# A hybrid decoder layer on one core: another place for the row of -M, for four blocks of weights and for the outputs' pool

## The chip, the core and the metric

The kernel runs on one NeuronCore of a Trainium2 chip. The core has a matrix engine (TensorE, in the profile PE, its weight loads PEld), a vector engine (VectorE, DVE), an engine for functions and copies (ScalarE, ACT), a small general engine (GpSimd, POOL) and one that issues transfers (SyncE, SP). They work side by side and wait for each other by semaphores. Each engine takes its own instructions strictly in the order in which the program lists them. The metric is the device time of one execution in microseconds. The kernel before was timed three times: 486.0, 486.98 and 487.39 us, median 486.98 us.

## What is computed

One layer of a decoder on 256 tokens with 1024 channels, all in float32. The mixer projects the input once into queries, keys and values of an mLSTM branch (4 heads) and of an attention branch (8 heads) and into gates; each branch is projected again, the two are gated, added and projected to the output. Then come a layer norm, a gated MLP with a convolution over three positions, and a second layer norm.

```python
def hybrid_mixer(x, w_in, b_in, conv_qk, mlstm_norm, rel_bias, w_branch_a, w_branch_b, w_out):
    proj = jnp.einsum("bsd,dn->bsn", x, w_in) + b_in
    q_m, k_m, v_m, o_m, i_m, f_m, q_b, k_b, v_b, g_a, g_b = _split_cols(proj, SPLIT_SIZES)
    qk = jax.nn.silu(causal_dwconv(jnp.concatenate([q_m, k_m], axis=-1), conv_qk))
    ...
    h_m = mlstm_chunkwise(q_m, k_m, v_m, i_m, f_m)
    y_a = sigmoid(o_m) * head_norm(h_m, mlstm_norm)
    h_b = moba_attention(q_b, k_b, v_b, rel_bias)
    merged = sigmoid(g_a) * (y_a @ w_branch_a) + sigmoid(g_b) * (h_b @ w_branch_b)
    return merged @ w_out
...
x = layer_norm(ALPHA * x + hybrid_mixer(x, ...), ln1_g, ln1_b)
u = causal_dwconv(x @ w_up, conv_ffn)
g, up = jnp.split(u, 2, axis=-1)
x = layer_norm(ALPHA * x + (silu(g) * up) @ w_down, ln2_g, ln2_b)
```

The mLSTM needs, for each head and each token, a running maximum M of gate sums. The kernel holds it as a row of -M over the 256 tokens, one row for each head.

## The kernel before

**Weights in chunks.** All weights come as 81 chunks of 1 MB (128 partitions x 2048 columns), in the order that `chunk_order` writes out: 4 chunks `o`, then four groups g = 0 to 3 of eight chunks each (`qm`, `qb`, `km`, `kb`, `vm`, `vb`, `ga`, `gb`, with the group's number behind: `vb3`), then `wa` and `wb` four times, `wo` four times, and the MLP's `up` and `dn`. Each chunk is loaded by SyncE into one of three buffers `raw`, cut by ScalarE into a high part `wh` and by VectorE into the rest `wl` (`split_into`), and multiplied on TensorE. Every product is made of three (`mm3`: high by high, high by low, low by high), so that a chunk is 8 blocks of input channels x 2 halves x 3 = 48 matmuls of 256 columns.

**Order.** The loop in `run` handles one chunk s at a time: it lists the element work of that step (`elem_work`: evacuation of the chunk before, side work of the attention and the mLSTM, the splitting of chunk s + 2), the load of chunk s + 5, then the 48 matmuls of s, then side products (`side_pe`). A table `mixed` sets the order of the element work where it is not the plain one. In group g the work of the step of `ga` matters here. On ScalarE and VectorE it has these pieces: `el_w` (for the mLSTM: from the row of -M, spread over 128 partitions in the tile `nMb`, two Exp activations make the weights `wt`; the table of the Exp function is loaded ahead of them, and GpSimd masks `wt` behind them), `el_l(0)` (attention scores `lg` and their maximum `mx` for the group's first head, on VectorE), the evacuation of `vb` (ScalarE copies the high part `vbh`, VectorE makes the rest `vbl`, ScalarE copies `vbf`; all three read the same tile in PSUM), `el_e(0)` (Exp of the scores), `el_s` (VectorE multiplies the products `pss` into `wt`, ScalarE copies the high part `sph`) and `el_s2` (VectorE makes the rest `spl`). Behind the 48 matmuls of `ga` TensorE runs `pe_l(1)` and then `pe_n`, the product `psn`, whose weight loads read `sph` and `spl`.

**The row of -M.** The gates' schedule ends with `e1d`: VectorE writes `nM`, and SyncE writes its four rows to HBM (`mrows`). `row_m` reads a group's row back, spread to 128 partitions, by a DMA that SyncE issues.

**Addresses.** The start of a tile within its partition, modulo 256 bytes, is chosen on purpose. `shift` sets at which of its columns a chunk's tile begins, so that what moves and what is loaded as weights start at chosen places. `odd` gives a few chunks a block that lies 8 columns (32 bytes) off the others: at the start (e), or the last n columns (z); its fourth value says whether the products begin with that block. The tile pool `y` holds the branches' outputs `yah`, `yal`, `ybh`, `ybl` and the gates; in the built program its tiles start at 224 modulo 256. During the first chunks `yah` and `yal` are borrowed for the split weights of chunk `o1`.

Of the kernel before, what the change touches and what calls it, by code (L numbers as in the profile page):

```python
# [18 lines left out]
P = 128  # L19
# [41 lines left out]
def shift(kind, i):  # L61

    if kind in ("vm", "vb", "o"):
        return 48
    if kind in ("wa", "wb"):
        return 56
    if kind == "dn":

        return 40
    return 0 if kind == "wo" else 16  # L70


class Kernel:
# [70 lines left out]
                self.mm3(ps[:, j, :], wh[:, a:a + P], wl[:, a:a + P], xh[:, k, :], xl[:, k, :], k == js[0],  # L144
                         k == js[-1])

    def mm_tok(self, s, ps, xh, xl, toks=(0, 1), kouter=False, ks=range(KT), first=None):
        todo = [(k, t) for k in ks for t in toks] if kouter else [(k, t) for t in toks for k in ks]
        for k, t in todo:
            c = slice(t * P, (t + 1) * P)  # L150
            a = self.col(s, k * 256)
            wh, wl = (w[:, a:a + 256] for w in self.w[s])
            self.mm3(ps[t], xh[:, k, c], xl[:, k, c], wh, wl, k == 0, k == KT - 1,
                     first if (k, t) == todo[0] else None)

    def ps_main(self, name):
        return self.psum.tile([P, 2, 256], F32, tag="mm", name=name, bufs=3)
# [4 lines left out]
    def run(self):  # L162
# [40 lines left out]
        self.yal = yp.tile([P, KT, S], F32R, name="yal")  # L203
        self.ybh = yp.tile([P, KT, S], F32R, name="ybh")
        self.ybl = yp.tile([P, KT, S], F32R, name="ybl")
        self.sigo = sigo = mp.tile([P, 2, D], F32, name="sigo")
        self.ident, self.vec = ident, vec

# [341 lines left out]
    def gates_schedule(self, bif):  # L550
# [38 lines left out]
        def e1d():  # L589
            fs, t1, F, G, M, nFM, nM = st["g"]  # L590
            v.tensor_scalar(self.nM[0:4, :], M, -1.0, None, op0=ALU.mult)
            v.scalar_tensor_tensor(nFM, F, -1.0, M, op0=ALU.mult, op1=ALU.subtract)
            st.update(G=G, nFM=nFM)
            nc.sync.dma_start(self.mrows, self.nM[0:4, :])

        def p1():
            ps = self.ps_side([P, 2, 2, 4], "ps_gc")
# [20 lines left out]
    def group_schedule(self, g):  # L618
# [185 lines left out]
            at(self.side_elem, 6, lambda: self.copy_band(g + 1))  # L804

        o = int(g < NG - 1)
        at(self.side_elem, 3 + o, row_m)
        at(self.side_pe, 4 + o, pe_s)
        at(self.side_pe, 4 + o, lambda: pe_l(0))
        at(self.side_pe, 5 + o, lambda: pe_l(1))  # L810
        at(self.side_pe, 5 + o, pe_n)
        if o:
            self.mixed[b + 6] = lambda w: [el_w, lambda: el_l(0), w[0], lambda: el_e(0), el_s, lambda: el_l2(0),
                                           el_s2] + w[1:]
        else:
            self.mixed[b + 5] = lambda w: [w[0], el_w, lambda: el_l(0), w[1], lambda: el_e(0), el_s,
                                           lambda: el_l2(0), el_s2] + w[2:]
# [165 lines left out]
    def step_up(self, s, i, *a):  # L983
        if i == 0:

            self.hid = {}
            self.pt_up = [self.ps_side([P, 2, S], f"ps_up{j}") for j in range(2)]
        if i < 2:
            for k in range(KT):
                if i == 0 and k == KT - 1:  # L990
                    self.x1_transpose(1, 0)
                for j in range(2):
                    self.mm_tok(s - i + j, [self.pt_up[j][:, t, :] for t in range(2)], self.x1h, self.x1l,
                                toks=(i,), ks=(k,))
            if i == 0:
                def trans():
                    self.x1_transpose(1, 1)
                    for h in range(2):
                        self.x1_split(1, h)
                self.side_pe.setdefault(s, []).append(trans)  # L1000
                return
            del self.w[s - 1], self.w[s]
            tu = self.fp.tile([P, 2, 2, S], F32, name="tu")

            def copy():
                for j in range(2):
                    self.nc.scalar.copy(tu[:, j], self.pt_up[j])

            def back():
                for j in range(2):  # L1010
                    ps = self.ps_side([P, 2, S], f"ps_upT{j}")
                    for f in range(2):
                        for t in range(2):
                            self.nc.tensor.transpose(ps[:, f, t * P:(t + 1) * P], tu[:, j, t, f * P:(f + 1) * P],
                                                     self.ident)
                    self.pt_up[j] = ps
            self.evac[s] = copy
            self.back = back
            self.up_parts = [self.up_evac(j, lambda j=j: self.pt_up[j]) for j in range(2)]
            return  # L1020
        ps = self.ps_main(f"ps_up{i}")
        self.mm_feat(s, ps, self.x1h, self.x1l, self.back if i == 2 else None)
        conv, gate = self.up_evac(i, lambda: ps)
        parts = [conv, None, None, gate]
        if i == 2:
            (a0, b0), (a1, b1) = self.up_parts
            parts = [a0, a1, conv, b0, None, None, b1, gate]
        self.evac[s] = parts
# [116 lines left out]
def odd(kind, i):  # L1145

    if kind == "kb":
        return 0, 8, 128, False
    if kind == "ga" and i < NG - 1:
        return 0, 8, 128, True  # L1150
    if (kind, i) == ("up", 2):
        return 0, 8, 256, True
    if (kind, i) in (("vb", 3), ("up", 0), ("up", 1)):
        return 8, 0, 0, False
    return 0, 0, 0, False

# [77 lines left out]
```

## Time and profile before

| | |
|---|---|
| median of three runs (lowest, highest) | 486.98 us (486.0, 487.39) |
| the profiled execution's own time | 486.63 us |
| its span, from the first to the last instruction | 484.9 us |
| TensorE busy, matmul / weight load | 98% / 95% |
| VectorE, ScalarE, GpSimd busy | 76%, 59%, 6% |
| mean granted TensorE clock | 0.995 |
| HBM read | 92.58 MB, 196 GB/s over the span |

The rows in the section on the trace are from that one profiled execution, in microseconds from the start of its span; 486.63 - 484.9 = 1.7 us lie around the span. Busy shares are means over the whole execution. TensorE's matmuls overlap: each is listed with about 0.28 us, but in an undisturbed chunk one starts every 0.113 us, so the time of a chunk is read from the start of its first matmul to the start of the one behind its last.

### The profile page before, as it was taken

Reading aid. Unit: us, or ns where it says so; the run is one execution under the profiler, and the core shown is the slowest. Engines: PE = TensorE matmul, PEld = TensorE weight load, DVE = VectorE, ACT = ScalarE, POOL = GpSimd, SP = SyncE. Lnnn points to the kernel's source line nnn. Section 1 sums busy time; section 2 is a strip of 40 time slices with the busy share of each in tenths; the row PEclk is TensorE's granted clock in tenths of the full one; section 3 lists DMA queues with packets and bytes.
Section 4 is the critical chain, followed back from the end, with each engine's and each line's share of the span. In section 5 each row is a group of like instructions: output and inputs, shape, how many; then the busy total and the mean of one; then the engine's idle time right before and its main releaser. Section 6 shows DMA issues by size and latency. Waiting matters only on the chain.

```text
span 484.9 us, 9423 instructions
## 1 busy us (share of the span) xinstructions
PE 475.6 (98%) x3832; PEld 459.8 (95%) x3832; DVE 370.5 (76%) x681; ACT 287.8 (59%) x499; POOL 27.7 (6%) x43
## 2 busy tenths in 40 slices
PE   8999999999999999999999999999999999999993
PEld 6999999999999999999999999999999999999983
DVE  4877986896689668985677788888668666866877
ACT  5578875686667766866654623767456544654530
POOL 0501011001100110002000001000000000000000
PEclk9999999999999999999999999999999999999998
DMA  6986676375636663653955581827464545455202
GB/s 214 314 299 180 224 257 203 109 272 190 213 106 254 191 213 95 230 210 109 388 199 173 180 342 43 304 90 261 175 224 170 214 175 196 174 218 194 88 1 88
DMA packets 20918, 94.29 MB, mean 194 GB/s; under 512 B 4837, under 2 KB 7793, under 8 KB 11017
## 3 DMA queue, kind: packets, MB, share of 16 engines
q1 hardware_dynamic: 16714, 87.61, 50.8%
q0 software_dynamic: 4160, 6.07, 4.0%
q8 instruction: 30, 0.49, 0.4%
q14 instruction: 14, 0.11, 0.1%
HBM read 92.58 MB, written 2.64 MB: 196 GB/s over the span
## 4 chain that ended last, share of the span: by engine, by line
PE 97%; DMA 1%; DVE 1%; issue 0%; SPq 0%; ACT 0%; DVEq 0%
PE ps_up L131 8%; PE ps_up L130 8%; PE ps_up L129 8%; PE ffn L131 4%; PE ffn L130 4%; PE ffn L129 4%; PE ps_vb L130 2%; PE ps_qm L129 2%; PE ps_gb L129 2%; PE ps_gb L131 2%; PE ps_vb L131 2%; PE ps_gb L130 2%; PE ps_ga L130 2%; PE ps_vb L129 2%; PE ps_kb L131 2%; PE ps_wb L131 2%
## 5 line engine op out<-in xcount | busy, mean ns | idle before, releaser
L94 DVE TENSOR_TENSOR wl<-raw,wh 128x1024 fp32r<-128x1024 f32 (+4 forms) x163 | 180.3, 1148 | 28.4 <-ACT wh L93 27.8
L93 ACT CAST wh<-raw 128x1024 fp32r<-128x1024 f32 (+4 forms) x163 | 153.1, 994 | 8.6 <-DMA raw<-in_wst_dram 6.2
L131 PE MATMUL ps_up<-x1h,wl 128*128 128x256 f32 x320 | 88.5, 276 | 0.0
L129 PE MATMUL ps_up<-x1h,wh 128*128 128x256 f32 x320 | 88.4, 276 | 0.0
L130 PE MATMUL ps_up<-x1l,wh 128*128 128x256 f32 x320 | 88.4, 276 | 0.0
L130 PEld LDWEIGHTS ps_up<-x1l,wh 128*128 128x128 f32 x320 | 60.1, 188 | 0.4
L129 PEld LDWEIGHTS ps_up<-x1h,wh 128*128 128x128 f32 x320 | 60.1, 188 | 0.3
L131 PEld LDWEIGHTS ps_up<-x1h,wl 128*128 128x128 f32 x320 | 60.1, 188 | 0.0
L1046 DVE SCALAR_TENSOR_TENSOR cu<-ps_up,vec,cu 128x255 f32<-128x255 f32 (+1 forms) x80 | 33.1, 476 | 23.2 <-ACT cu L1042 23.2
L131 PE MATMUL ffn<-wh,hl 128*128 128x512 f32 (+1 forms) x94 | 35.5, 378 | 0.0
L130 PE MATMUL ffn<-wl,hh 128*128 128x512 f32 (+1 forms) x94 | 35.5, 377 | 0.0
L129 PE MATMUL ffn<-wh,hh 128*128 128x512 f32 (+1 forms) x94 | 35.3, 375 | 0.0
L93 ACT CAST hh<-cu 128x256 fp32r<-128x256 f32 x22 | 8.9, 407 | 43.2 <-DVE cu L1054 43.2
L1042 ACT ACTIVATE cu<-ps_up,vec 128x256 f32<-128x256 f32 x40 | 16.7, 469 | 25.6 <-PE ps_up L131 25.6
L131 PEld LDWEIGHTS ffn<-wh,hl 128*128 128x128 f32 x94 | 17.7, 188 | 3.2
L129 PEld LDWEIGHTS ffn<-wh,hh 128*128 128x128 f32 x94 | 17.7, 188 | 3.1
L130 PEld LDWEIGHTS ffn<-wl,hh 128*128 128x128 f32 x94 | 17.7, 188 | 3.1
L129 PE MATMUL ps_qm<-xth,wh 128*128 128x256 f32 x64 | 18.1, 282 | 0.0
L129 PE MATMUL ps_ga<-xth,wh 128*128 128x256 f32 x64 | 18.0, 281 | 0.0
L130 PE MATMUL ps_vb<-wl,xth 128*128 128x256 f32 x64 | 17.9, 279 | 0.0
L129 PE MATMUL mix<-wh,mgh 128*128 128x256 f32 x64 | 17.8, 279 | 0.0
L129 PE MATMUL ps_gb<-xth,wh 128*128 128x256 f32 x64 | 17.8, 279 | 0.0
(319 smaller groups left out, 1439.6 us busy)
## 6 DMA issues: line engine op xcount, KB each, us to landing
raw<-in_wst_dram SPq DMA_DIRECT2D x77, 1024.0 KB, 4.9
raw<-in_wst_dram SPq DMA_DIRECT2D x8, 256.0 KB, 4.7
lnrow<-in_rows_dram POOLq DMA_DIRECT2D x4, 512.0 KB, 6.6
band<-table POOLq DMA_DIRECT2D x4, 384.0 KB, 12.8
xraw<-in_xt_dram SPq DMA_DIRECT2D x8, 128.0 KB, 4.1
toe<-band POOLq DMA_DIRECT2D x4, 256.0 KB, 3.6
xtok<-in_x_dram POOLq DMA_DIRECT2D x1, 1024.0 KB, 7.5
sgb<-in_wst_dram SPq DMA_DIRECT2D x4, 128.0 KB, 3.8
```

Of the source, the lines that this page charges most:

```text
L93: self.nc.scalar.copy(wh, raw)
L94: self.nc.vector.tensor_sub(wl, raw, wh.bitcast(F32))
L129: mm(ps, ah if first is None else first, bh, start=start, stop=False)
L130: mm(ps, ah, bl, start=False, stop=False)
L131: mm(ps, al, bh, start=False, stop=stop)
L1042: act.activation(cu[:, j, :], ps[:, j, :], AF.Copy, scale=tap(2, j))
L1046: v.scalar_tensor_tensor(cu[:, j, o:], ps[:, j, :S - o], tap(t, j), cu[:, j, o:], op0=ALU.mult, op1=ALU.add)
```

## The change

Four things change. (1) SyncE reads group 0's row of -M back directly behind the DMA that writes the rows; the rows of the other groups are read in the step of `qb` of their group, earlier than before. In groups 0 to 2 `el_w` stands behind the evacuation of `vb` in the table `mixed`, where it stood first. (2) In `vb3` the block that lies off is now the last one, moved by 32 bytes the other way, and the first half of the products begins with it; the second half ends with it. (3) In the second token half of the first two `up` chunks, the products begin with block 1 and end with block 0, the one that lies off. (4) A pad of 40 columns in the pool `y` puts its tiles at 64 modulo 256 in place of 224, and `shift` gives `wa` and `wb` the common 16 columns in place of 56.

```diff
@@ -62,8 +62,6 @@

     if kind in ("vm", "vb", "o"):
         return 48
-    if kind in ("wa", "wb"):
-        return 56
     if kind == "dn":

         return 40
@@ -144,14 +142,19 @@
                 self.mm3(ps[:, j, :], wh[:, a:a + P], wl[:, a:a + P], xh[:, k, :], xl[:, k, :], k == js[0],
                          k == js[-1])

-    def mm_tok(self, s, ps, xh, xl, toks=(0, 1), kouter=False, ks=range(KT), first=None):
+    def mm_tok(self, s, ps, xh, xl, toks=(0, 1), kouter=False, ks=range(KT), first=None, ends=(0, KT - 1)):
         todo = [(k, t) for k in ks for t in toks] if kouter else [(k, t) for t in toks for k in ks]
-        for k, t in todo:
+        if odd(*self.order[s])[3]:
+
+            todo = todo[KT - 1:KT] + todo[:KT - 1] + todo[KT:]
+        for n, (k, t) in enumerate(todo):
             c = slice(t * P, (t + 1) * P)
             a = self.col(s, k * 256)
             wh, wl = (w[:, a:a + 256] for w in self.w[s])
-            self.mm3(ps[t], xh[:, k, c], xl[:, k, c], wh, wl, k == 0, k == KT - 1,
-                     first if (k, t) == todo[0] else None)
+            start, stop = (k == edge for edge in ends)
+            if odd(*self.order[s])[3]:
+                start, stop = n % KT == 0, n % KT == KT - 1
+            self.mm3(ps[t], xh[:, k, c], xl[:, k, c], wh, wl, start, stop, first if n == 0 else None)

     def ps_main(self, name):
         return self.psum.tile([P, 2, 256], F32, tag="mm", name=name, bufs=3)
@@ -203,6 +206,8 @@
         self.yal = yp.tile([P, KT, S], F32R, name="yal")
         self.ybh = yp.tile([P, KT, S], F32R, name="ybh")
         self.ybl = yp.tile([P, KT, S], F32R, name="ybl")
+
+        yp.tile([P, 40], F32, name="ypad")
         self.sigo = sigo = mp.tile([P, 2, D], F32, name="sigo")
         self.ident, self.vec = ident, vec

@@ -592,6 +597,7 @@
             v.scalar_tensor_tensor(nFM, F, -1.0, M, op0=ALU.mult, op1=ALU.subtract)
             st.update(G=G, nFM=nFM)
             nc.sync.dma_start(self.mrows, self.nM[0:4, :])
+            self.row_m[0]()

         def p1():
             ps = self.ps_side([P, 2, 2, 4], "ps_gc")
@@ -804,13 +810,16 @@
             at(self.side_elem, 6, lambda: self.copy_band(g + 1))

         o = int(g < NG - 1)
-        at(self.side_elem, 3 + o, row_m)
+        if g:
+            at(self.side_elem, 1, row_m)
+        else:
+            self.row_m = [row_m]
         at(self.side_pe, 4 + o, pe_s)
         at(self.side_pe, 4 + o, lambda: pe_l(0))
         at(self.side_pe, 5 + o, lambda: pe_l(1))
         at(self.side_pe, 5 + o, pe_n)
         if o:
-            self.mixed[b + 6] = lambda w: [el_w, lambda: el_l(0), w[0], lambda: el_e(0), el_s, lambda: el_l2(0),
+            self.mixed[b + 6] = lambda w: [lambda: el_l(0), w[0], el_w, lambda: el_e(0), el_s, lambda: el_l2(0),
                                            el_s2] + w[1:]
         else:
             self.mixed[b + 5] = lambda w: [w[0], el_w, lambda: el_l(0), w[1], lambda: el_e(0), el_s,
@@ -986,12 +995,14 @@
             self.hid = {}
             self.pt_up = [self.ps_side([P, 2, S], f"ps_up{j}") for j in range(2)]
         if i < 2:
-            for k in range(KT):
+
+            ks = list(range(KT)) if i == 0 else list(range(1, KT)) + [0]
+            for k in ks:
                 if i == 0 and k == KT - 1:
                     self.x1_transpose(1, 0)
                 for j in range(2):
                     self.mm_tok(s - i + j, [self.pt_up[j][:, t, :] for t in range(2)], self.x1h, self.x1l,
-                                toks=(i,), ks=(k,))
+                                toks=(i,), ks=(k,), ends=(ks[0], ks[-1]))
             if i == 0:
                 def trans():
                     self.x1_transpose(1, 1)
@@ -1148,9 +1159,11 @@
         return 0, 8, 128, False
     if kind == "ga" and i < NG - 1:
         return 0, 8, 128, True
+    if (kind, i) == ("vb", 3):
+        return 0, 8, 256, True
     if (kind, i) == ("up", 2):
         return 0, 8, 256, True
-    if (kind, i) in (("vb", 3), ("up", 0), ("up", 1)):
+    if (kind, i) in (("up", 0), ("up", 1)):
         return 8, 0, 0, False
     return 0, 0, 0, False

```

On ScalarE in group 0, before (`wh` is the last weight split ahead, `gcol` to `wt` is `el_w`, `vbh` and `vbf` the evacuation of `vb`; a row's end names the engines or DMA queues whose semaphores it waits for):

```order
L93 CAST wh_790<-raw_599 128x1024 [waits DMAHW7_49,PE_49]
L93 CAST wh_790<-raw_599 128x1024
L606 COPY gcol<-ps_gc 128x8 [waits PE_49]
L644 ACT_TABLE_LOAD [waits DMASW4_49,DMAHW1_49,Activation_49]
L644 ACTIVATE wt_884<-nMb,gcol 128x128 [waits Pool_49]
L645 ACTIVATE wt_884<-nMb,gcol 128x256
L93 CAST vbh<-ps_vb_801 128x256
L508 COPY vbf<-ps_vb_801 128x256 [waits DVE_49]
L756 ACTIVATE lg_888,sm_890<-lg_888,mx_889 128x128
L756 ACTIVATE lg_888,sm_890<-lg_888,mx_889 128x256
L657 CAST sph_900<-wt_884 128x384 [waits DVE_49]
```

After:

```order
L91 CAST wh_791<-raw_601 128x1024 [waits DMAHW0_49,PE_49]
L91 CAST wh_791<-raw_601 128x1024
L91 CAST vbh<-ps_vb_802 128x256 [waits PE_49]
L513 COPY vbf<-ps_vb_802 128x256 [waits DVE_49]
L612 COPY gcol<-ps_gc 128x8 [waits PE_49]
L650 ACT_TABLE_LOAD [waits DMASW4_49,DMAHW7_49,Activation_49]
L650 ACTIVATE wt_894<-nMb,gcol 128x128 [waits Pool_49]
L651 ACTIVATE wt_894<-nMb,gcol 128x256
L762 ACTIVATE lg_882,sm_884<-lg_882,mx_883 128x128
L762 ACTIVATE lg_882,sm_884<-lg_882,mx_883 128x256
L663 CAST sph_901<-wt_894 128x384 [waits DVE_49]
```

The two copies of `vb` have moved ahead of `gcol`, the load of the Exp table and the two Exps. Groups 1 and 2 change in the same way (without `gcol`). VectorE's order is the same in both kernels there: `lg`, `mx`, `vbl`, `wt`, ..., `spl`.

On SyncE around the row of -M of group 0, before (`raw` are weight loads, `mrows` the writing, `nMb` the reading):

```order
L88 DMA raw_529<-in_wst_dram 128x2048 [waits DMAHW5_49,DMAHW2_49,DVE_49]
L594 DMA mrows<-nM 4x256 [waits DVE_49]
L88 DMA raw_599<-in_wst_dram 128x2048 [waits DMAHW3_49,Activation_49]
L88 DMA raw_672<-in_wst_dram 128x2048 [waits DMAHW4_49,DVE_49]
L625 DMA nMb<-mrows 128x256 [waits DMAHW6_49]
L88 DMA raw_738<-in_wst_dram 128x2048 [waits DMAHW5_49,DVE_49]
```

After:

```order
L86 DMA raw_530<-in_wst_dram 128x2048 [waits DMAHW5_49,DMAHW2_49,DVE_49]
L599 DMA mrows<-nM 4x256 [waits DVE_49]
L631 DMA nMb<-mrows 128x256 [waits DMAHW6_49]
L86 DMA raw_601<-in_wst_dram 128x2048 [waits DMAHW3_49,Activation_49]
L86 DMA raw_674<-in_wst_dram 128x2048 [waits DMAHW4_49,DVE_49]
L86 DMA raw_739<-in_wst_dram 128x2048 [waits DMAHW5_49,DVE_49]
```

The reading of the row has moved ahead of two weight loads.

## Rows read from the trace of the kernel before

**Rows 1.** the page's chain that ended last: share of the span, by engine
```profile
PE 97%; DMA 1%; DVE 1%; issue 0%; SPq 0%; ACT 0%; DVEq 0%
```

**Rows 2.** waits of TensorE's weight loads: line, awaited, us in total, times, longest
```profile
PEld ps_vb L130 <- DVE wl L94: 0.2, 1, 0.2
```

**Rows 3.** stretches, products of gb0 and gb1: us, busy (count), clock, DMA share, GB/s
```profile
72.26:77.91 5.65, 5.65 (x48) 1.00 0.61 149
121.75:127.21 5.46, 5.46 (x48) 1.00 0.63 220
```

**Rows 4.** stretches, products of vb2 and vb3
```profile
156.74:162.18 5.44, 5.44 (x48) 1.00 0.56 194
207.69:213.44 5.75, 5.75 (x48) 1.00 0.45 180
```

**Rows 5.** ScalarE timeline, group 0: start us, us, engine, line, operation, tiles
```profile
63.79 1.99 ACT L93 CAST wh<-raw 128x1024 fp32r<-128x1024 f32 x2
65.68 0.15 ACT L606 COPY gcol<-ps_gc 128x8 f32<-128x8 f32 x1
65.90 1.28 ACT L644 ACT_TABLE_LOAD   x1
...
68.75 0.37 ACT L508 COPY vbf<-ps_vb 128x256 f32<-128x256 f32 x1 [0.49 <-DVE vbl L94]
69.02 0.40 ACT L756 ACTIVATE lg<-lg,mx 128x128 f32<-128x128 f32 x1
```

**Rows 6.** VectorE timeline, group 0
```profile
67.81 0.17 DVE L749 TENSOR_SCALAR mx<-mx 128x2 f32<-128x2 f32 x1
...
68.63 0.55 DVE L653 SCALAR_TENSOR_TENSOR wt<-pss,wt 128x384 f32<-128x384 f32 x1
...
70.70 0.55 DVE L663 TENSOR_TENSOR spl<-wt,sph 128x384 fp32r<-128x384 f32 x1
```

**Rows 7.** VectorE timeline, group 1
```profile
115.51 0.17 DVE L749 TENSOR_SCALAR mx<-mx 128x2 f32<-128x2 f32 x1
115.59 0.42 DVE L94 TENSOR_TENSOR vbl<-ps_vb,vbh 128x256 fp32r<-128x256 f32 x1
```

**Rows 8.** ScalarE timeline, group 1
```profile
116.04 0.38 ACT L508 COPY vbf<-ps_vb 128x256 f32<-128x256 f32 x1 [2.04 <-DVE vbl L94]
```

**Rows 9.** VectorE timeline, group 3
```profile
209.33 0.55 DVE L653 SCALAR_TENSOR_TENSOR wt<-pss,wt 128x384 f32<-128x384 f32 x1
...
210.55 0.55 DVE L663 TENSOR_TENSOR spl<-wt,sph 128x384 fp32r<-128x384 f32 x1
```

**Rows 10.** weight load of spl in the timeline, group 0
```profile
71.31 0.19 PEld L131 LDWEIGHTS psn<-vmh,spl 128*128 128x128 f32 x1
```

**Rows 11.** SyncE timeline, issues around the row of -M
```profile
52.82 0.28 SPq L594 DMA_DIRECT2D mrows<-nM  x1
...
58.71 0.43 SPq L625 DMA_DIRECT2D nMb<-mrows  x1
```

**Rows 12.** DMA issues: tiles, engine, count, KB each, median us to landing
```profile
raw<-in_wst_dram SPq DMA_DIRECT2D x77, 1024.0 KB, 4.9
...
nMb<-mrows SPq DMA_DIRECT2D x4, 128.0 KB, 4.9
```

**Rows 13.** weight load of spl in the timeline, group 1
```profile
120.80 0.19 PEld L131 LDWEIGHTS psn<-vmh,spl 128*128 128x128 f32 x1
```

**Rows 14.** stretches, products of up0 to up2
```profile
295.19:299.30 4.11, 4.11 (x38) 1.00 0.01 4
301.52:306.83 5.31, 5.31 (x47) 1.00 0.63 194
306.83:309.66 2.83, 2.83 (x26) 1.00 0.97 391
```

**Rows 15.** stretches of six output-gate products each, TensorE
```profile
12.37:13.73 1.36, 1.36 (x8) 1.00 0.88 235
17.95:19.36 1.41, 1.41 (x9) 1.00 1.00 304
```

## Prediction

> **What bounds the kernel now.** I read the chain of waits first. The reader is to see that 97% of it is TensorE [rows 1]: what ends the kernel is the sum of the starts of TensorE's matmuls, and other engines count only where TensorE waits for them. Next come the waits of its weight loads. The reader is to see how little they hold: the one among the four groups that the list names is 0.2 us in front of vb0, for VectorE's split of that chunk [rows 2]. So there is hardly anything to win by moving work on the other engines, and much to lose: what comes late for TensorE is paid in full. Third I read stretches of TensorE, chunk by chunk. Chunks of the same 48 products take 5.65 us in gb0 and 5.46 us in gb1, at the full granted clock in both [rows 3], and 5.44 us in vb2 and 5.75 us in vb3 [rows 4]. Per product that is 113 to 114 ns in the quick ones and about 118 ns in the slow ones. This is the second place where the change can act. Last I read the timelines of ScalarE and VectorE in group 0 between 63 and 72 us, where the order changes.
>
> **The order on ScalarE in group 0.** No instruction is added or removed. Behind the splits that run from 63.79 us, ScalarE took gcol at 65.68 and the load of the Exp table at 65.90; the copy vbf came after the Exps and waited 0.49 us for VectorE's vbl [rows 5]. Now vbh and vbf stand ahead of gcol, and VectorE's order is the same as before. So vbf still waits for vbl, and vbl still stands behind the scores' maximum mx, which VectorE does at 67.81 [rows 6]. Queued behind the waiting vbf are gcol, the table's load, both Exps, GpSimd's mask, and with them wt, sph and spl, for which TensorE waits in psn. Step by step:
>
> - vbl starts 0.08 us after mx starts (115.51 to 115.59 [rows 7]): 67.81 + 0.08 = 67.89. In the old order the same copy needed vbh, which came later; that gain is in this number.
> - vbf starts 0.45 after vbl (115.59 [rows 7] to 116.04 [rows 8]): 68.34.
> - gcol starts 0.27 after vbf (as the next instruction does, 68.75 to 69.02), the load 0.22 after gcol (65.68 to 65.90) [rows 5]: 68.83, which is 2.93 us later than 65.90.
> - VectorE's wt follows the load by at most 68.63 - 65.90 = 2.73 us [rows 5, 6]: 71.56. Some hundredths less are possible, since VectorE had vbl in front of it then.
> - From wt to spl VectorE needs 210.55 - 209.33 = 1.22 us where nothing else holds it [rows 9]: 72.78 in place of 70.70 [rows 6], 2.08 later.
>
> TensorE's weight load of spl started at 71.31, right at the end of spl (70.70 + 0.55 = 71.25) [rows 6, 10]. It waited for spl already, so all of the 2.08 us shifts TensorE, and nothing behind it gives time back, because TensorE has no idle time to use. I take +2.0 us, with bounds +1.8 and +2.2.
>
> On this chain the Trainium skill, ScalarE: Activation LUTs, "What ACT_TABLE_LOAD costs", says that each switch to another set of functions costs about 1.28 us for the load and about 1.38 us for a drain, together 2.66 us. The row has the 1.28, but no room for a drain: gcol starts 0.22 us ahead of the load [rows 5]. By the row the term is 2.0 us; by the page, with a drain in front of the moved load, it would be 3.4 us.
>
> **The row of -M.** In group 0 the reading of the row went out at 58.71 [rows 11] and takes 4.9 us to land [rows 12]: 63.6 us, 2.3 us before the load of the Exp table that waits for it. Reading it earlier saves nothing; what hides it is ScalarE's own queue. What it could cost: SyncE now waits for the landing of the writing, issued at 52.82, and two weight loads are queued behind it. At worst the writing takes the 4.9 us that the larger reading takes: the reading is issued at about 57.8, the first weight load at 58.2 after the 0.43 us of that issue [rows 11], and lands 4.9 us later [rows 12], at 63.1. ScalarE's splits of that chunk start at 63.79 [rows 5], so 0.7 us are left: cost 0, bound +0.5 if both transfers slow each other. In groups 1 to 3 the reading is only issued earlier, ahead of two or three weight loads, each put off by the 0.43 us of an issue: 0.
>
> **The order in groups 1 and 2.** There is no gcol. vbf runs from 116.04 to 116.42 [rows 8], the table's load behind it at 116.42, wt at most 2.73 later at 119.15, spl at 120.37, its end (0.55) at 120.92. TensorE's weight load could follow 0.06 later, at 120.98; it now starts at 120.80 [rows 13]. That is 0.1 to 0.2 us late. The old order had over two us of cover here, the new one has none. What is late next is the spacing: in gb0, behind such a wait, the products kept the slow spacing for the whole chunk, in gb1, without one, they did not, 5.65 against 5.46 us [rows 3]. So each of the two groups costs 0.15 + 0.19 = 0.34, together +0.68; bounds 0 (spl comes just in time) and +1.0.
>
> **The odd blocks.** vb3 takes 0.31 us more than vb2 [rows 4]; a part of that is the restart behind the full-float32 product psl, which vb2 does not have. The new block is to bring the quick spacing. What a block in another place does to the spacing, no row shows; bounds -0.31 and 0, I take -0.2. In the second token half of up0 and up1, 45 products took 5.31 us (118.0 ns), in the first half 36 took 4.11 (114.2 ns), and the first 24 of up2 took 2.83 (117.9 ns) [rows 14] (the counts in the rows include one or two that were still running). At 114.2 ns these 69 would take 0.26 us less. The six products with the odd block now stand at the end and will be slow in any case: bounds -0.26 and +0.1, I take -0.2.
>
> **The outputs' pool.** Six output-gate products took 1.41 us with their weights in yah, 1.36 us with a tile at 64 [rows 15]: four such blocks, 0.2 us. But this comes before vb0, where TensorE waits for VectorE [rows 2], whose work there is fed by weights that arrive and not by TensorE. The 0.2 us become a longer wait: 0, bound -0.2. The eight chunks wa and wb keep the distance between what moves and what is loaded (64 modulo 256, before from 224 to 32, now from 64 to 128), and the places 64 and 128 are those of gb1 with its 5.46 us: 0; if they went slow, 8 x 0.19 = +1.5 us.
>
> **Sum.** 2.0 + 0.68 - 0.2 - 0.2 = +2.28 us. Made against the profiled execution's own 486.63 us (span 484.9 and 1.7 around it) this is 488.9; that execution lies 0.35 us under the median of the runs, so for the median I add it to 486.98: 489.3 us.
>
> **Rivals.**
> - Not slower, because vbf does not hold the queue. If the values' copy in group 0 started at once behind vbh, at about 66.1, gcol and the load would come at about 66.6, less than a us later than before, spl at about 70.5 or, behind VectorE's own work, at its old place. Then the 2.0 and the 0.68 fall away: 486.98 - 0.4 = 486.6. For it: vbh comes earlier now. Against it: vbf waited for vbl in both groups shown, 0.49 and 2.04 us [rows 5, 8], and vbl stays behind mx. It decides at the start of vbf: before 66.5, or at 68.3.
> - The wait is as computed, but the rest goes better: groups 1 and 2 just in time, the odd blocks at their full 0.57, gb0 quick again (-0.19): +1.24, 488.2, inside 0.3%.
> - The places go wrong: the odd blocks gain nothing, wa and wb run slow: 2.0 + 0.68 + 1.5 = 4.2, 491.2 us. Against it: the same places run quick in gb1 [rows 3].
> - A drain stands in front of each moved table load in groups 0 to 2. 1.4 us more in each: 2.28 + 4.2 = 6.5, 493.5 us. Against it are the 0.22 us in front of the load [rows 5]. It is the sum to which the page's rule above leads.
>
> **How the numbers follow.** My forecast, 488.4 to 490.2, has 0.75; not slower 0.06; better rest 0.09; wrong places 0.07; the drain 0.01. The 0.02 left go to faster by more than 0.3%, about 1.46 us, which is what a measurement of this kernel can tell from no change; all gains at their bounds come to 1.2, so no sum that I have reaches it. Slower by over 0.3% (above 488.44): 0.75, 0.07 and 0.01, less 0.02 at the forecast's lower edge, 0.81. Within: 0.06 + 0.09 + 0.02 = 0.17. The range from 487.9 to 490.8 takes in the better rest and a part of the wrong places.
>
> **What would show it.** Right: in group 0 vbf starts at about 68.3 with gcol, the load and the Exps behind it, wt at 71.5, spl at 72.8, and the weight load of spl at 73.3, with a wait of TensorE of nearly 2 us in front of psn that was not listed before; in groups 1 and 2 the weight load of spl starts at the end of spl, and gb1 and gb2 take 5.65 us; vb3 takes about 5.55, the second half of up0 and up1 about 0.2 less; wa and wb are unchanged. Wrong: vbf before 66.5, a spl that TensorE does not wait for, or a chunk at 118 ns that was at 113.

## The result and the profile after

The changed kernel takes 490.39 us (median of 6 runs, 489.75 to 490.53) where the kernel before took 486.49 (6 runs beside it, 485.95 to 487.39). The ratio is 1.0074, with a 95% interval from 1.0063 to 1.0085: 3.1 to 4.1 us slower. The forecast was 489.3, the range 487.9 to 490.8. So the direction and the range held, but the time lies above the likeliest case's own range (488.4 to 490.2): the sum of 2.3 us was too small by 1.3, since the ratio makes it 3.6. (The two medians differ by 3.9. Differences in us below are worked out from the ratios, on 486.5 us, where nothing else is said.)

The profiled execution of the changed kernel took 490.43 us, its span is 488.7, the mean granted clock 0.997. First the chain that ended last, by engine, which answers to [rows 1]:

```profile
PE 81%; DVE 3%; ACT 1%; issue 1%; POOL 0%; DVEq 0%; POOLq 0%
```

The shares add up to 86% only: followed back, the chain leaves TensorE at the wait for yt ahead of psy0, goes on over ScalarE, GpSimd and VectorE to the load of the Exp table in group 0, and is followed no further back than 69.5 us. Most of the fall from 97% to 81% is this missing stretch (69.5 of 488.7 us are 14%) and no measure of the waits. (psy0 stands for TensorE's transposes of `yt`, the mLSTM's output of group 0, behind the chunk qm1.) The waits of the weight loads (what waits, line, for whom: us in total, times, longest) name the place, and answer to [rows 2]:

```profile
PEld psn L127 <- ACT sph L663: 3.0, 1, 3.0
...
PEld psn L129 <- DVE spl L669: 0.4, 1, 0.4
...
PEld psy L724 <- ACT yt L718: 0.3, 1, 0.3
```

One wait of 3.4 us in group 0, and a new one of 0.3 at psy0. Before, the list named neither. The weight load of spl in group 0 starts at 74.11 where it started at 71.31 [rows 10]:

```profile
74.11 0.19 PEld L129 LDWEIGHTS psn<-vmh,spl 128*128 128x128 f32 x1 [0.42 <-DVE spl L669]
```

ScalarE's timeline in group 0, from vmh to sph (start, duration, operation, then the idle time before it and what ended it), answers to [rows 5]:

```profile
62.53 0.62 ACT L91 CAST vmh<-vtmp 128x512 fp32r<-128x512 f32 x1 [2.30 <-DVE vtmp L499]
64.50 2.00 ACT L91 CAST wh<-raw 128x1024 fp32r<-128x1024 f32 x2 [1.35 <-DMA raw<-in_wst_dram]
66.41 0.36 ACT L91 CAST vbh<-ps_vb 128x256 fp32r<-128x256 f32 x1
69.06 0.37 ACT L513 COPY vbf<-ps_vb 128x256 f32<-128x256 f32 x1 [2.29 <-DVE vbl L92]
69.33 0.17 ACT L612 COPY gcol<-ps_gc 128x8 f32<-128x8 f32 x1
69.57 1.28 ACT L650 ACT_TABLE_LOAD   x1
...
72.83 0.51 ACT L663 CAST sph<-wt 128x384 fp32r<-128x384 f32 x1 [0.29 <-DVE wt L659]
```

VectorE's timeline beside it answers to [rows 6]:

```profile
68.53 0.17 DVE L755 TENSOR_SCALAR mx<-mx 128x2 f32<-128x2 f32 x1
68.61 0.42 DVE L92 TENSOR_TENSOR vbl<-ps_vb,vbh 128x256 fp32r<-128x256 f32 x1
72.24 0.56 DVE L659 SCALAR_TENSOR_TENSOR wt<-pss,wt 128x384 f32<-128x384 f32 x1 [3.21 <-POOL wt L652]
...
73.52 0.54 DVE L669 TENSOR_TENSOR spl<-wt,sph 128x384 fp32r<-128x384 f32 x1
```

Two things stand there. The wait of vbf for vbl, 2.29 us, is the one that was forecast, with gcol, the table's load and the Exps behind it. The other was not forecast: 1.35 us of ScalarE's idle time ahead of the split at 64.50, for a weight load. SyncE's issues show why (answering to [rows 11]):

```profile
52.09 0.28 SPq L599 DMA_DIRECT2D mrows<-nM  x1
...
56.18 0.33 SPq L631 DMA_DIRECT2D nMb<-mrows  x1
...
56.60 0.38 SPq L86 DMA_DIRECT2D raw<-in_wst_dram  x1
57.59 0.33 SPq L86 DMA_DIRECT2D raw<-in_wst_dram  x1
```

For 4.1 us, from 52.09 to 56.18, SyncE waits for the writing of the rows to land. The weight load that the split at 64.50 reads goes out at 56.60, with the next one a microsecond behind it. Before, it went out directly behind the writing, with the next one 5.1 us behind it (two issues in one row):

```profile
53.19 5.47 SPq L88 DMA_DIRECT2D raw<-in_wst_dram  x2
```

In windows of the same stretch the columns behind the duration are the clock, the busy share of the DMA engines and GB/s; first the kernel before:

```profile
54.00:58.00 4.00, 1.00 0.80 297
...
62.00:64.00 2.00, 1.00 0.67 196
```

then the changed one:

```profile
54.00:58.00 4.00, 1.00 0.08 30
...
62.00:64.00 2.00, 1.00 1.02 420
```

The DMA engines are almost idle while SyncE waits (busy share 0.08), and are then full (1.02) with loads that came together: the load issued at 56.60 takes 7.8 us to land, those issued at 61.92 and 67.97 take 8.2 and 6.8, where the median of all is 4.9 [rows 12].

Stretches of TensorE, chunk by chunk, as in [rows 3, 4]: gb0 and vb3, then qb1, km1 and kb1, the three chunks behind psy0 (start and end, us, busy and count, clock, DMA share, GB/s):

```profile
75.06:80.52 5.46, 5.46 (x48) 1.00 0.57 131
...
211.66:217.22 5.56, 5.56 (x48) 1.00 0.49 181
...
88.64:94.29 5.65, 5.65 (x50) 1.00 0.29 81
94.29:99.95 5.66, 5.66 (x51) 1.00 0.42 171
99.95:105.61 5.66, 5.66 (x51) 1.00 0.59 204
```

Added up over TensorE's starts, the first trace of after against that of before: the chunks `o` and vb0 -0.6, the products psn of group 0 +3.4, gb0 -0.2, psy0 +0.35, qb1 to kb1 +0.6 (before: 5.45, 5.44 and 5.47), psn of groups 1 and 2 +0.34, vb3 -0.18; together 3.7 of the 3.8 us between the two spans.

### The profile page after: what moved, and what is told of

The parts are those of the page before. It is cut to its first block, busy times and chain, and to the rows that moved or that the text cites. A ratio compares the mean times of both kernels' runs of the same rounds, so it can differ in the third digit from the quotient of the medians.

```text
span 488.7 us, 9423 instructions
## 1 busy us (share of the span) xinstructions
PE 475.7 (97%) x3832; PEld 459.5 (94%) x3832; DVE 369.8 (76%) x681; ACT 287.9 (59%) x499; POOL 28.0 (6%) x43
## 4 chain that ended last, share of the span: by engine, by line
PE 81%; DVE 3%; ACT 1%; issue 1%; POOL 0%; DVEq 0%; POOLq 0%
PE ps_up L129 8%; PE ps_up L127 8%; PE ps_up L128 8%; PE ffn L129 4%; PE ffn L128 4%; PE ffn L127 4%; PE mix L127 1%; PE ps_wa L127 1%; PE ps_wb L127 1%; PE mix L129 1%; PE mix L128 1%; PE ps_wa L128 1%; PE ps_wa L129 1%; PE ps_wb L129 1%; PE ps_wb L128 1%; PE ps_kb L129 1%
## 5 line engine op out<-in xcount | busy, mean ns | idle before, releaser
L127 PE MATMUL ps_qb<-xth,wh 128*128 128x256 f32 x64 | 17.8, 279 | 0.0
L129 PE MATMUL ps_kb<-xth,wl 128*128 128x256 f32 x64 | 17.8, 278 | 0.0
```

Of the source, the lines that this page charges most:

```text
L127: mm(ps, ah if first is None else first, bh, start=start, stop=False)
L129: mm(ps, al, bh, start=False, stop=stop)
```

## The experiments

All ratios are to runs of the kernel before on the same chip.

**The two suspects, each undone and each alone.** The diffs: `old_order` is the whole change with `mixed` as it was, `old_rows` the whole change with `row_m` as it was, `row_alone` and `order_alone` the kernel before with one of the two put in.

```diff
 # order_alone (old_order: the reverse, from the changed kernel)
-            self.mixed[b + 6] = lambda w: [el_w, lambda: el_l(0), w[0], lambda: el_e(0), ...
+            self.mixed[b + 6] = lambda w: [lambda: el_l(0), w[0], el_w, lambda: el_e(0), ...
 # row_alone (old_rows: the reverse, from the changed kernel)
-        at(self.side_elem, 3 + o, row_m)
+        if g:
+            at(self.side_elem, 1, row_m)
+        else:
+            self.row_m = [row_m]      # called behind the writing of mrows
```

> The kernel before with only the new order in groups 0 to 2. Theory, as recorded: vbf starts at about 68.3, spl's weight load at 73.3, +2.0 in group 0; groups 1 and 2 0.15 us each, the chunk gb behind them at either spacing: 486.5 + 2.1 to 2.7 = 488.6 to 489.2 us. Rival (the order has most of the 3.9 us itself, by the late pow of group 0 and the slow chunks behind it, and the row none): 490 us or more.

Measured: 489.46 us, ratio 1.0059 (1.0040 to 1.0078), +2.9 us (1.9 to 3.8). ScalarE in its trace:

```profile
62.89 1.99 ACT L93 CAST wh<-raw 128x1024 fp32r<-128x1024 f32 x2
64.78 0.36 ACT L93 CAST vbh<-ps_vb 128x256 fp32r<-128x256 f32 x1
67.44 0.37 ACT L508 COPY vbf<-ps_vb 128x256 f32<-128x256 f32 x1 [2.29 <-DVE vbl L94]
```

The theory's 2.1 to 2.7 lie inside, and so does the rival's 490 us (1.0072): the time alone does not part them. In this trace the rival's mechanism is absent, since psy0 does not wait and qb1 to kb1 are quick (5.45, 5.44 and 5.47 us). The split follows vmh with no wait, and vbf waits by the same 2.29 us. spl starts at 71.89, 9.00 us behind the start of the split; before it was 6.91 (63.79 to 70.70 [rows 5, 6]), in the whole change it is 9.02. So the new order makes this chain 2.1 us longer, with the row moved or not. VectorE's spl:

```profile
71.89 0.54 DVE L663 TENSOR_TENSOR spl<-wt,sph 128x384 fp32r<-128x384 f32 x1
```

> The kernel before with only the reading of the row moved, in all groups. Theory: ScalarE's split at 63.8 waits for its load by about 1.3 us, and gcol, the table's load, wt and spl behind it come as much later: 486.5 + 1.3 = 487.8 us. Rival (recorded step: 0, at most +0.5): 486.5 to 487.0.

Measured: 487.56 us, ratio 1.0019 (1.0008 to 1.0029), +0.9 us (0.4 to 1.4). The theory's 1.3 lies inside; the rival's 0 does not, but its upper bound of +0.5 just does. The split at 64.61 has 1.03 us of idle time ahead of it, where it had next to none before:

```profile
64.61 2.00 ACT L93 CAST wh<-raw 128x1024 fp32r<-128x1024 f32 x2 [1.03 <-PE psl L131]
```

The row names a product of TensorE as what ended it; but the load that this split reads, issued at 57.05, took 7.5 us and so landed at about 64.5, right ahead of the split. TensorE then waits 0.6 us each for sph and spl.

> The changed kernel with the old order in groups 0 to 2 (el_w first); the early reading of the row, the blocks and the pool stay. Theory (the change lost by two things in group 0: vbf holds gcol and the table's load behind the scores' maximum, and the reading of the row, waiting on SyncE for the writing, holds the weight load behind it so that ScalarE splits that chunk 1.35 us late): only the first goes. ScalarE's split at 64.5 still waits for its load, TensorE's weight load of spl starts at about 72.0 in place of 74.1, the pow of group 0 and the slow chunks behind it go back in part: 486.6 to 487.6 us where the kernel before has 486.5. Rival (the order is the only loss, the late load is hidden in the old order): 485.6, faster than before by the blocks and the pool.

Measured: 486.90 us, ratio 1.0004 (0.9995 to 1.0013). The split still waits 1.03 us for its load, TensorE 0.6 us each for sph and spl:

```profile
64.39 2.00 ACT L91 CAST wh<-raw 128x1024 fp32r<-128x1024 f32 x2 [1.03 <-DMA raw<-in_wst_dram]
```

The rival's 485.6 (0.9982) is out: the order is not the only loss.

> The changed kernel with the row of -M read at its old places; the new order, the blocks and the pool stay. Theory: the weight load goes out behind the writing again, ScalarE's split does not wait, mx, vbl, vbf and the table's load all come 1.35 us earlier, spl's weight load at about 72.8: 490.4 - 1.35 = 489.0 us, 488.6 if the pow of group 0 is in time again. Rival (my recorded step: the early reading costs nothing, since vbf waits for the scores' maximum in any case): 490.4, as with the whole change.

Measured: 488.87 us, ratio 1.0048 (1.0030 to 1.0066), with the split at 63.30 directly behind vmh and TensorE's wait at psn down from 3.4 us to 2.1. The rival's 490.4 (1.0080) is out. (The whole change's interval begins at 1.0063, so the two intervals just touch; the waits in the traces say the same as the medians.)

**What in the reading costs: the queue.** `row_gpsimd` is the whole change, with group 0's row read by GpSimd's queue.

```diff
-            nc.sync.dma_start(self.nMb, self.mrows[g:g + 1, :].to_broadcast([P, S]))
+            q = nc.sync if g else nc.gpsimd
+            q.dma_start(self.nMb, self.mrows[g:g + 1, :].to_broadcast([P, S]))
```

> The whole change, with group 0's row of -M read by GpSimd's queue in place of SyncE's, at the same place behind its writing. Theory (the early reading costs because SyncE waits 4 us for the writing to land and the next weight load stands behind it in its queue): the load goes out right behind the writing, at about 52.6, ScalarE's split behind vmh does not wait, 488.6 to 489.0 us, as with the row at its old places. Rival (the reading itself, as one more transfer, slows the weight loads): ScalarE's split waits as before, 490.4 us.

Measured: 489.00 us, ratio 1.0053 (1.0038 to 1.0067). Both values of the theory (1.0043 and 1.0051) lie inside, the rival's 490.4 does not. The load goes out right behind the writing, and the split no longer waits. SyncE, then ScalarE, of its trace:

```profile
52.72 0.27 SPq L599 DMA_DIRECT2D mrows<-nM  x1
53.09 5.47 SPq L86 DMA_DIRECT2D raw<-in_wst_dram  x2
...
63.17 0.62 ACT L91 CAST vmh<-vtmp 128x512 fp32r<-128x512 f32 x1 [2.31 <-DVE vtmp L499]
63.69 1.99 ACT L91 CAST wh<-raw 128x1024 fp32r<-128x1024 f32 x2
```

GpSimd issues the reading at 57.91, 5.2 us behind the writing: 1.1 us later than in the whole change and 0.7 earlier than before. As one more transfer beside the loads it costs nothing that the time shows (489.00 against the 488.87 of `old_rows`); it is the wait in SyncE's queue ahead of the load that costs. The Trainium skill, DMA: Bandwidth & Descriptors, "Issuing engines are not separate DMA queues", says that issuing from another engine saves only the time that the issuing takes, which is mostly small. This case's traces show the other half: what stood in the queue was not an issue of 0.43 us but a wait of 4.1, and moving the waiting read to another engine gave back 1.0 us by the ratios (1.0074 to 1.0053), 1.4 by the medians.

**What in the order costs: one copy.** `vbf_behind` is the kernel before with the new order, but with vbf as a piece of its own behind el_w.

```diff
-            self.split_into(h, l, ps[:, 0, :])
-            nc.scalar.copy(f, ps[:, 1, :])
-        self.evac[s] = evac
+            self.split_into(h, l, ps[:, 0, :])
+        self.evac[s] = [evac, lambda: nc.scalar.copy(f, ps[:, 1, :])]
...
-            self.mixed[b + 6] = lambda w: [el_w, lambda: el_l(0), w[0], ...
+            self.mixed[b + 6] = lambda w: [lambda: el_l(0), w[0], el_w, w[1], ...
```

> The kernel before with the new order in groups 0 to 2, but with the last copy of the evacuation, vbf, behind el_w: ScalarE takes vbh, gcol, the table's load, both Exps and then vbf. Theory (vbf's wait for VectorE's vbl, 2.3 us, is what the new order costs): the load starts 0.4 us behind vbh as in the old order, spl at most 0.3 later than in the old one: 486.4 to 486.9 us. Rival (the evacuation ahead of the load costs, or the table's load in its new place): 488 us or more, as with the whole new order.

Measured: 486.09 us, ratio 0.9994 (0.9984 to 1.0005). The rival is out. ScalarE in group 0:

```profile
66.68 0.36 ACT L93 CAST vbh<-ps_vb 128x256 fp32r<-128x256 f32 x1
66.95 0.17 ACT L605 COPY gcol<-ps_gc 128x8 f32<-128x8 f32 x1
67.18 1.28 ACT L643 ACT_TABLE_LOAD   x1
...
69.34 0.37 ACT L508 COPY vbf<-ps_vb 128x256 f32<-128x256 f32 x1
```

Within the interval (-0.8 to +0.2 us) the whole loss of the order is the wait of this one copy, which holds four instructions that TensorE needs: without it ahead of them, TensorE's list shows no wait at psn.

**The places.** `no_row_order` is the kernel before with the blocks and the pool alone, `pool_alone` with the pool and `shift` alone.

```diff
 # both
-    if kind in ("wa", "wb"):
-        return 56
+        yp.tile([P, 40], F32, name="ypad")
 # no_row_order alone, beside the new order of up's blocks
+    if (kind, i) == ("vb", 3):
+        return 0, 8, 256, True
```

> The kernel before with only the parts on places: vb3's and up's blocks and the outputs' pool. Theory as recorded: vb3 -0.2, the pool nothing, up -0.2: 486.1 us where the kernel before has 486.5. By what the four kernels run so far showed (vb3 5.57 us in place of 5.75 wherever the new block is in, up without a difference, and about 0.6 between each pair with and without these parts): 485.9 us; then the pool gives about 0.3 to 0.4. Rival (these parts give nothing but vb3's 0.18): 486.3.

Measured: 486.28 us, ratio 0.9989 (0.9980 to 0.9998): -0.5 us (-1.0 to -0.1). All three values named in advance (486.1, 485.9 and 486.3) lie inside; the time does not tell them apart.

> The kernel before with only the outputs' pool at 64 and wa, wb at the common 16 columns. Theory, as recorded: nothing to -0.2 us, 486.4, wa and wb at the same 5.45 us or so each. Rival (the pool has what vb3 and up leave of the 0.5 us of the kernel with the places alone, and more): 486.2 or less.

Measured: 486.40 us, ratio 1.0003 (0.9993 to 1.0012): no difference that could be measured; the rival's 486.2 (0.9994) is still just inside. In all 14 traces each of the eight chunks wa and wb takes 5.44 or 5.45 us.

**Second traces.** `before_again` and `after_again` are the two kernels with no edit, for another trace of each.

> The kernel before once more, for a second trace of it. Theory: its first trace had late first loads by chance (ScalarE's first cut of a whole chunk at 27.0 us, in the five other traces so far at 26.1 to 26.7) and one slow chunk, gb0, by chance; a second trace shows the cut at 26.1 to 26.7, no wait of TensorE in front of vb0 (5.53 us in place of 5.81), and another set of slow chunks. Rival: late cut, wait at vb0 and the slow gb0 belong to the kernel before and show again.

Measured: one execution, 487.34 us. The cut came at 27.58, so the theory's early cut is a miss. The rest holds: vb0 takes 5.53 us and gb0 5.46, and other chunks have the slow spacing. The stretches of qb0, km0 and kb0 in this trace, where that of before had 5.54, 5.44 and 5.47 us:

```profile
35.82:41.55 5.73, 5.73 (x51) 1.00 0.91 295
41.55:47.20 5.65, 5.65 (x50) 1.00 0.27 86
47.20:52.86 5.66, 5.66 (x50) 1.00 0.72 213
```

> The changed kernel once more, for a second trace. Theory: what the program sets shows again: ScalarE's split waits for its load by about 1 us, spl's weight load at about 74, vb3 5.57 us. What the first trace had by chance need not: slow qb1, km1 and kb1, up0 and up1 at 6.04 us, and the clock at 1.2 GHz for some us behind the wait in psn may show instead (1.4 us in the kernel with the early pow). Rival: the slow qb1 to kb1 follow from the wait at psy0 and show whenever that does.

Measured: one execution, 490.73 us. The split at 63.87 waits 0.59 us for its load (about 1 was expected), spl's weight load comes at 73.48 (74 was expected), vb3 takes 5.56. There is no wait at psy0, and qb1, km1 and kb1 are quick. In their place stands the clock. Windows of this trace behind the wait at psn (us, busy and count, clock, DMA share, GB/s):

```profile
72.00:74.00 2.00, 1.02 (x5) 0.90 0.09 14
74.00:76.00 2.00, 2.00 (x11) 0.50 0.24 51
76.00:78.00 2.00, 2.00 (x15) 0.74 0.90 103
78.00:80.00 2.00, 2.00 (x19) 1.00 0.60 244
```

From 74 to 76 the clock is 0.50 of full speed, 1.2 GHz, behind a stretch in which TensorE waited 2.6 us at psn; psn and gb0 take 1.7 us longer than in the first trace (8.8 against 7.1). In the first trace, behind a wait that was longer by 0.8 us, the clock stayed at 1.00.

**The late pow.** In the first trace of the changed kernel, GpSimd's pow of group 0 begins at 85.14, 4.6 us behind its input (80.41 + 0.17), and ScalarE's yt, for which TensorE waits at psy0, behind it. That the pow is late is not peculiar to this trace: in all 13 traces without an earlier pow it begins 2.2 to 4.6 us behind its input, and the pows of the later groups 0.1 behind theirs. Only in this one does psy0 wait. GpSimd's queue shows what stands ahead of the first pow and of no later one (first trace of after, then that of `early_pow`; behind the durations in ns stand the starts of the first and the last of them):

```profile
L711 POOLq MODIFY_POOL_CONFIG  x2: 37/37/37, 73.5 to 73.5; - x2
...
L603 POOLq MODIFY_POOL_CONFIG  x2: 8/8/8, 57.8 to 57.8; - x2
```

In the 13 traces they follow the masking of wt and the issue of one DMA, and in all 14 the first pow begins 9.8 to 11.6 us behind them. So a late wt makes this pow late: the two stand at 73.5 in the first trace of after, and at 69.9 in that of before, with the pow at 80.43. That the pow waits for them is read from this distance and from `early_pow`, which puts them at 57.8. `early_pow` puts a pow of two columns on GpSimd far ahead of it.

```diff
             self.row_m[0]()
+            w = self.nM[32:64, 0:2]
+            nc.gpsimd.memset(w, 1.0)
+            nc.gpsimd.tensor_tensor(w, w, self.mhalf[32:64, :], op=ALU.pow)
```

> The whole change, with a pow of two columns on GpSimd behind the gates, which nobody reads, so that what GpSimd loads ahead of its first pow comes at about 57 us and not in group 0's norm. Theory (in the changed kernel this load took 4.6 us between scl at 80.58 and the pow at 85.14, yt came late by it and TensorE waited 0.35 us in front of psy0): the pow starts within 0.3 us of scl, no wait at psy0: 490.0 us, and 489.4 if the slow qb1, km1 and kb1 were its consequence. Rival (GpSimd was held by the issue of the band's DMA): the pow stays at 85, 490.4 us.

Measured: 490.85 us, ratio 1.0094 (1.0080 to 1.0109): no faster than the whole change (1.0074, 1.0063 to 1.0085). GpSimd in its trace:

```profile
57.70 0.09 POOL L602 MEMSET nM<- 32x2 f32 x1
69.11 0.73 POOL L603 TENSOR_TENSOR nM<-nM,mhalf 32x2 f32<-32x2 f32 x1 [11.32 <-ACT gcol L615]
...
80.27 1.65 POOL L714 TENSOR_TENSOR scl<-scl,mhalf 128x2 f32<-128x2 f32 x1 [7.06 <-DVE scl L713]
```

The pow is as expected: the second one starts 0.1 us behind its input, psy0 has no wait, qb1 to kb1 are quick (as they are in `after_again` too, with no early pow). The time is a miss: the clock fell to 1.2 GHz behind psn, psn and gb0 took 1.7 us longer, and the mean clock was 0.991 or 0.992 in each of the four runs. The two MODIFY_POOL_CONFIG have moved ahead with the first pow, which begins 11.3 us behind them (the releaser named in its row, gcol, is not an input). What GpSimd does in that time the rows don't show; that it loads something, as the expectation has it, stays open.

**What is left when both losses are out.** `places_and_vbf` is `no_row_order` with the edit of `vbf_behind`.

> The parts on places (blocks, pool) with the old reading of the row, and the new order with vbf behind el_w: what is left of the change when its two losses are taken out. Theory (the two add up: -0.3 to -0.5 from the places, 0 to -0.4 from the order with vbf behind): 485.7 to 486.3 us, faster than the kernel before. Rival: the places alone are as good or better, 486.3 us.

Measured: 485.87 us, ratio 0.9988 (0.9980 to 0.9997), 0.6 us faster than the kernel before (0.1 to 1.0). It beats both kernels, but it is not to be told from the places alone (0.9989).

## Why the prediction was right, and where it was wrong

- **The order in group 0: right.** The forecast from the split to spl was 72.78 - 63.79 = 8.99 us; the traces have 9.02 and 9.00. vbf started 0.45 us behind vbl, the load 0.51 behind vbf, wt 2.67 behind the load (2.73 was the upper bound). The rival by which vbf does not hold the queue fell by the 2.29 us of its wait, and `vbf_behind` shows that this wait is the whole of it.
- **No drain at the table's load.** By the Trainium skill, ScalarE: Activation LUTs, "What ACT_TABLE_LOAD costs", a drain of about 1.38 us would have stood ahead of each moved load. It does not: the load in group 0 starts 0.24 us behind the start of gcol, which itself takes 0.17.
- **The row of -M: wrong, and the larger error.** The step that failed is "cost 0, bound +0.5". It rested on two numbers. The landing of the writing was not the trouble: the reading was issued at 56.18, earlier than the 57.8 taken. But the load behind it was given the median 4.9 us [rows 12] (the two loads of that stretch had taken 5.5 before), and landed at about 64.4, some 7.8 us behind its issue. The next load followed it by 1 us, and the DMA engines moved 420 GB/s; that sharing them is what made it late is argued from this, and no run spaces the two loads. The cover of 0.7 us was gone and 1.35 us stood on the path (0.53 to 1.35 in the five traces that have this issue order). Alone this cost 0.9 us (0.4 to 1.4), and within the whole change, by `old_rows` and `row_gpsimd`, 1.3 and 1.0 by the ratios, 1.5 and 1.4 by the medians.
- **Groups 1 and 2: the wait right, the spacing wrong.** psn took 0.19 and 0.15 us longer, 0.15 each were forecast. But gb1 and gb2 kept 5.46 us in the first trace. In the six traces with the new order gb1 was slow twice (in none of the eight others), gb2 never, and gb0 was slow at the full clock in one kernel with the wait and in two without. So this wait does not set the slow spacing; whether it makes it likelier, as gb1 may hint, is not shown. The 0.19 each, read from one trace, came in two of twelve chunks.
- **vb3: right.** 5.56 or 5.57 us in all eight traces with the new block, 5.75 in all six without: -0.18 for -0.2.
- **up: about right in size, not in this trace.** From the start of up0's second half to the end of up3 it takes 17.94 us in the first trace of before and 17.95 in that of after. With the new place it takes 17.78 in five of eight traces, without it 17.94 or more in all six. So the gain is 0.17 where it comes, and both traces of the changed kernel have none of it.
- **The pool and wa, wb: right,** 0 within what can be measured. The -0.3 us that the first trace of after has in vb0 is not the pool's: the second trace of before has it too.
- **What no step had.** The longer wait of TensorE is followed by a cost of its own, in one of two forms: either the clock falls to 1.2 GHz behind it (1.7 us in the second trace and in `early_pow`), or, in the first trace, psy0 waits for the late pow, which a late wt sets, and three chunks run slow (0.95 us). The runs without a trace point to the clock too: a mean clock of 0.991 or 0.992 stands in ten of the 28 timed executions that have vbf ahead of the Exps, and in none of the 69 of the other kernels or the 67 of the kernel before, whose lowest is 0.994. (A mean of 0.994 does not rule the fall out: the second trace of the changed kernel has both.) In `order_alone` the two with 0.991 took 491.03 and 491.07 us, the other four 488.21 to 489.83, so that a part of its +2.9 is likely the clock and not the wait itself. That the slow chunks follow from psy0 is not shown: they went together in one trace, and chunks run slow without it elsewhere.

The parts add up: the order +2.9, the row +0.9, the places -0.5 make +3.3, the whole change +3.6 (3.1 to 4.1). Of the 1.3 us by which 3.6 exceeds the forecast's sum of 2.3, the row explains 0.9 to 1.5; the clock stands in the measured cost of the order, and its share is not worked out.

The closeness is in part luck. The forecast was made against 486.98 us, and the runs beside the changed kernel have 486.49: against these the same sum gives 488.8, and the range would have ended at 490.3, below the measured 490.39 (as a ratio the range ends at 1.0078, and 1.0074 is inside). And the 0.38 taken for a slow gb1 and gb2 stood in the sum where the row's 0.9 or more was missing. One sum can't be followed: "all gains at their bounds come to 1.2"; the bounds given for vb3, up and the pool make 0.77, with a quick gb0 0.96. Only a chance of 0.02 hung on it.

## What to carry to other kernels

A DMA that waits for another one's landing holds every load behind it in its queue for that time (4.1 us here), and the loads that then go out together can land later than their median says (7.8 against 4.9 us): give such a read to a queue with nothing urgent behind it. On an engine that takes its work in order, an instruction with no hurry must not stand, with its wait, ahead of those that the bounding engine needs; cut the piece apart and move the one copy. A difference of a chunk or of an early stretch that stands in one trace only is not yet a property of the program: a second trace of the same kernel costs little.

## What was not expected of the hardware

- The same program runs 48 equal products in 5.46 or in 5.65 us, in other chunks in each execution: gb0 in one trace of before, qb0 to kb0 in the other, at the full granted clock in all.
- Behind waits of TensorE in psn of 2.6 to 3.4 us in all, the clock fell to 1.2 GHz in two of three traces, and not in the one with the longest wait. Behind the waits of 1.7 to 2.1 us in the traces of `order_alone`, `old_rows` and `row_gpsimd` it stayed at 1.00.
- The first of two 1 MB loads issued about 1 us apart landed after 7.2 to 7.8 us in five traces, with the DMA engines at about 420 GB/s, against 4.9 us for the median of all loads.
- GpSimd's first pow of the kernel started 2.2 to 4.6 us behind its input in 13 traces, later ones 0.1 behind theirs. In all 14 it started 9.8 to 11.6 us behind two MODIFY_POOL_CONFIG in GpSimd's queue, which stand ahead of no later pow.
